# A two-layer hybrid encoder: the chunked attention's queries and keys by a seven-fold block product through DRAM, and one item of filler to a differential step

## The chip, the cores and the metric

The kernel runs on one core of one Trainium2 chip. The metric is the device time in microseconds of one execution. Before the change three runs gave 1897.2, 1899.48 and 1903.69 us, median 1899.48 us.

## The reference, cut to what matters

`x` has one batch of 512 rows of 1024 channels. Two layers follow each other; each has a token mixer of three branches on the same input, and a gated feed-forward net. All of it is float32.

```python
def _token_mixer(x, w_in, ...):
    rq, rk, rv, rg, cq, ck, cv, dq, dk, dv, gate = split(x @ w_in)   # widths below
    a = _retention(rq, rk, rv, rg) @ w_branch_a          # 4 heads
    b = _chunk_attention(cq, ck, cv, rel_bias) @ w_branch_b   # 8 heads of 64
    c = _diff_attention(dq, dk, dv, lam) @ w_branch_c    # 4 heads, 2 score maps of 64 each
    y = sigmoid(gate[0]) * a + sigmoid(gate[1]) * b + sigmoid(gate[2]) * c
    return y @ w_out
```

`cq`, `ck`, `cv`, `dq`, `dk` and `dv` are 512 columns wide, each gate 1024. In the chunked attention a chunk of 64 queries sees its own and the eight chunks before it, with a bias by clipped distance, a softmax and a product with the values. In the differential attention queries and keys are first turned by rotary positions; each head makes two softmax maps, subtracts the second times lambda from the first, multiplies by the values and normalises each row.

## The kernel before, in words

**Numbers.** A float32 operand is carried as two parts, a high one (a rounded copy, made by ACT) and a low one (the remainder, made by DVE); names end in `h` and `l`. A product is three matmuls into one PSUM bank, high by high, high by low, low by high (`mm3`, L122 to L125). Weights come as float32 by DMA into one of four staging buffers (`st`) and are split into `wh` and `wl` (class `Wt`, L128 to L157; the cast L155 is ACT's, the subtraction L156 DVE's), each in two halves. Three buffers of each sort hold the weights of three items at a time (`AHEAD` is 3). Most other tiles come from a pool of 61 slots of 128x512.

**Items and groups.** The mixer is written as a list of items (the table at L1095 to L1115 of before). An item is one weight, or a few, with the matmuls on it: nearly always two halves of 24 matmuls each. Behind an item's name stand groups of steps. Each call of `between` takes the next group: the first group runs between the halves of the item, the second at its end. So PE's order is the order of this table, and every other engine has its work queued in the order in which the table emits it; a scheduler moves instructions a little within that. When an item is emitted, the weights of the next ones are fetched and split, so their casts stand in ACT's and DVE's queues about two items early, and each waits until the buffer of an older weight has been read for the last time.

**Products of block matrices.** `u_two` (L716) computes two projections of 512 columns each by seven block products in place of eight (items `a` and `c` set up the operands; the items `m1, m2, y, x, g, h, v` are the products). An item has 48 matmuls 256 columns wide. It is used for the values of both attentions (`w`: CV and DV) and for the retention's values and gates (`p`, `q`). What `w` makes is stored in DRAM (`v_away`) and fetched again ahead of use (`v_back`).

**Queries and keys.** `u_cqk(p)` projects the queries and keys of one pair of chunked heads, as two halves of 24 matmuls 512 columns wide, four items a layer; `QK.set_q` and `set_k` (L361 on) split them into `qs`, `ks` and `kl`. `u_dqk(h)` does this for a differential head, with the rotary between (`rotary`, L345 on: four copies of 32 rows by ACT, L352, and three operations by DVE, L354 to L356).

**Steps.** `s_c1, s_c2, s_c3` are the steps of a chunked head: scores (L387, L388), row operation (DVE L402), exponentials (ACT L404), normalisation (DVE L899); transposes and split; product with the values (L924) and output `ob` (L926, L927 and the split). For a differential head `s_d0` makes scores and exponentials of one map, `s_d1` at its second map the combination `dE` (DVE, L964 to L970), `s_d2` the transposes (`ptr`) and their split, `s_d3` the product with the values (`pdo`), squares, POOL's power (L1011) and scalings (L1014), `s_d4` the transposes `pdt` and the output `oc`. `c(i)` and `d(i)` put them into groups, so that the steps of neighbouring heads overlap. Before, an odd step `d(2h+1)` and the next even one had an item with no steps between them (`u_dqk(1)`, `u_dqk(2)`, `u_dqk(3)`).

**Gates and branches.** `u_gate` projects 256 columns of a gate; the gates in `EARLY` (six of twelve) go to DRAM (`th`) and come back in `gate_of`. `u_branch(br, i)` multiplies a branch's output (`oa`, `ob`, `oc`) by its weight and adds it, gated, to the sum (L1065, L1069).

Of the kernel before, what the change touches and what calls it, by code (L numbers as in the profile page):

```python
# [12 lines left out]
F32 = mybir.dt.float32  # L13
# [4 lines left out]
P = 128  # L18
# [26 lines left out]
EARLY = [(0, 0), (0, 1), (0, 2), (0, 3), (2, 0), (2, 1)]  # L45
# [12 lines left out]
def trunk(ctx, tc, x_in, xT_in, w_in, ret_norm_g, da_norm_g, lq1, lk1, lq2, lk2, w_a, w_b, w_c, b_merge, w_out,  # L58
# [68 lines left out]
    class Wt:  # L127


        def __init__(self, pieces, nk, later=False):  # L130
# [230 lines left out]
    class QK:  # L361
# [21 lines left out]

        def scores(self, ps, j, nt):

            w, n = P * (nt + 1), slice(P * nt, P * nt + P)
            nc.tensor.matmul(ps[:, :w], self.q[j][:, n], self.k[j][:, :w], start=True, stop=False)  # L387
            nc.tensor.matmul(ps[:, :w], self.q[j][:, n], self.kl[j][:, :w], start=False, stop=True)  # L388
# [134 lines left out]

    def run_items():
        ready, at = [], 0

        def fetch():
            nonlocal at
            specs, at = items[at][0], at + 1
            ready.append([])  # L530
            if at == 1:
                ready[-1] += first_blocks(*specs)
                return
            for sp in specs:
                ready[-1].append(sp() if callable(sp) else Wt(*sp))

        for i, (specs, fn, groups) in enumerate(items):
            while at <= i or (at < len(items) and sum(map(len, ready)) < AHEAD):
                fetch()
# [37 lines left out]
    def layer(l):  # L577
# [138 lines left out]
        def u_two(left, right, left_done, right_done):  # L716
# [5 lines left out]
            def it(name, use):  # L722
                def fn(wt):
                    for j in range(2):
                        use(j, functools.partial(product, xq, name, j, wt))
# [158 lines left out]
        def s_c1(h):  # L884
            def fn():
# [168 lines left out]

        def u_branch(br, i):
# [3 lines left out]
            def fn(wt):  # L1059
                act = (oa, ob, oc)[br]  # L1060
                for j in range(2):
                    d = 2 * i + j
                    t = gate_of(br, d)
                    ps = proj_T(act, wt, P * j, nk=nk)
                    nc.vector.scalar_tensor_tensor(t, t, 1.0, ps, op0=ALU.add, op1=ALU.mult)  # L1065
                    if br == 0:
                        acc[d] = t
                    else:
                        nc.vector.tensor_add(acc[d], acc[d], t)  # L1069
                    if br == 2:  # L1070
                        mg[d] = Pair("mg")
                        split(mg[d], acc.pop(d), scale=0.5)
                    between()
            return [([w[:, 256 * i:256 * i + 256]], nk)], fn

# [17 lines left out]

        w, p, q = u_two(CV, DV, v_away(cv, 64), v_away(dv, 128, -1.0)), u_rvg(0), u_rvg(1)
        for (specs, fn), *groups in [  # L1095
            (u_first(), [w["a"]]), (u_gate(0, 1), [w["c"], s_q(0)], [s_q(1)]), (u_gate(0, 2), [s_q(2)], [s_q(3)]),
            (w["m1"],), (w["m2"], [lam]), (w["y"],), (w["x"],), (w["g"],), (u_gate(0, 3), [p["a"]], [s_dh(0)]), (w["h"],),
            (w["v"], [p["c"]]),
            (p["m1"], [], [s_r1(0)]), (p["m2"], [s_dh(1)]), (p["y"], [], [s_r1(1)]), (p["x"],), (p["g"],),
            (u_rqk(rq, RQ, 1), [q["a"]]), (p["h"],), (p["v"], [q["c"]]),  # L1100
            (q["m1"], [], [s_r2(0)]), (u_rqk(rk, RK, 1), [s_r2(1)], [s_r3(0)]), (q["m2"], [], [s_r3(1)]), (q["y"], [s_dh(2)]),
            (q["x"], [], [s_r1(2)]), (q["g"], [s_dh(3)]), (u_cqk(0), [], [s_r1(3)]), (q["h"],), (q["v"],),
            (u_gate(2, 0), [s_r2(2)], [s_r2(3), s_r3(2)]), (u_cqk(1), [s_r3(3)] + c(0)[0], c(0)[1]),
# [411 lines left out]
```

## Time and profile before

| | |
|---|---|
| median of the three runs | 1899.48 us |
| the profiled execution's own time | 1898.38 us |
| its span | 1896.5 us |
| granted TensorE clock, mean | 0.999 |
| PE, DVE, ACT, POOL busy | 99%, 72%, 50%, 6% |
| DMA | 297.84 MB, mean 157 GB/s |
| waits of PE in all | 14 us |

A row of the groups has the line, the engine, the operation, the tiles written and read, their shape, the count, then busy us and the mean ns of one, then the idle time of the engine ahead of them and what released it. A row of the windows has the stretch in us from the span's start, its length, and for PE, PEld, DVE, ACT and POOL the busy us with the number of instructions, then the granted clock, the mean busy share of the DMA engines and GB/s. A row of the timeline has start, length, engine, line, operation, tiles. In the first layer the differential steps run from about 399 to 534 us, the products of the third branch to 556 us; the second layer repeats them some 940 us later.

### The profile page before, as it was taken

How to read it: one execution, taken by the hardware profiler on the slowest of the kernel's cores; microseconds unless marked ns; L12 is line 12 of the kernel's file. 1: busy time of each engine (PE TensorE's matmuls, PEld its weight loads, DVE VectorE, ACT ScalarE, POOL GpSimd, SP SyncE). 2: the span in 40 equal slices, each digit the busy share in tenths (PEclk: the TensorE clock that was granted, in tenths of full speed). 3: DMA queues.
4: the chain of work that ended last, by engine and by line, in shares of the span. 5: the costliest groups of instructions: out<-in, count | busy, mean ns of one | idle time of the engine just before them, and what ended most of it. 6: DMA issues, size and time to landing. Idle time of an engine off the chain costs nothing. (4 is left out here: it accounts for less than half of the span.)

```text
span 1896.5 us, 26422 instructions
## 1 busy us (share of the span) xinstructions
PE 1873.9 (99%) x10354; PEld 1630.4 (86%) x10354; DVE 1358.4 (72%) x2065; ACT 957.4 (50%) x1547; POOL 105.5 (6%) x117
## 2 busy tenths in 40 slices
PE   9999999999999999999999999999999999999998
PEld 7788888888888999988898888888888889999886
DVE  5877766667766877787587777566776678877866
ACT  4644555567644444444255546455765344444431
POOL 0000000000001000010000010000000010000100
PEclk9999999999999999999999999999999999999999
DMA  8685443332156387885546835433322654869851
GB/s 264 193 255 141 142 142 127 109 117 87 56 169 187 105 231 177 240 209 151 156 167 195 241 110 166 159 112 97 122 71 80 199 129 145 211 157 266 206 149 45
DMA packets 221745, 297.84 MB, mean 157 GB/s; under 512 B 9534, under 2 KB 116148, under 8 KB 221620
## 3 DMA queue, kind: packets, MB, share of 16 engines
q1 hardware_dynamic: 198388, 250.01, 39.9%
q0 software_dynamic: 23232, 46.14, 14.0%
q8 instruction: 81, 1.33, 0.3%
q14 instruction: 44, 0.36, 0.1%
HBM read 273.00 MB, written 23.12 MB: 156 GB/s over the span
## 5 line engine op out<-in xcount | busy, mean ns | idle before, releaser
L123 PE MATMUL pt<-xTh,wh 128*128 128x512 f32 (+1 forms) x1456 | 506.9, 349 | 1.3 <-ACT wh L261 1.3
L124 PE MATMUL pt<-xTl,wh 128*128 128x512 f32 (+1 forms) x1456 | 502.5, 345 | 2.1 <-DVE xTl L113 1.9
L125 PE MATMUL pt<-xTh,wl 128*128 128x512 f32 (+1 forms) x1456 | 502.1, 345 | 0.0
L262 DVE TENSOR_TENSOR wl<-st,wh 128x2048 fp32r<-128x2048 f32 x126 | 288.1, 2289 | 135.0 <-ACT wh L261 134.7
L261 ACT CAST wh<-st 128x2048 fp32r<-128x2048 f32 x126 | 240.0, 1910 | 227.4 <-PE pt L124 129.1
L124 PEld LDWEIGHTS pt<-xTl,wh 128*128 128x128 f32 x1456 | 276.1, 190 | 34.5 <-DVE xTl L113 2.3
L123 PEld LDWEIGHTS pt<-xTh,wh 128*128 128x128 f32 x1456 | 275.7, 190 | 34.8 <-ACT wh L261 1.7
L125 PEld LDWEIGHTS pt<-xTh,wl 128*128 128x128 f32 x1456 | 275.7, 189 | 34.0
L155 ACT CAST wh<-st 128x1024 fp32r<-128x1024 f32 (+1 forms) x204 | 188.1, 948 | 195.6 <-issue 71.1
L156 DVE TENSOR_TENSOR wl<-st,wh 128x1024 fp32r<-128x1024 f32 (+1 forms) x204 | 219.0, 1095 | 90.6 <-ACT wh L155 84.2
L123 PE MATMUL pf<-wh,hqh 128*128 128x512 f32 x224 | 87.5, 391 | 0.5 <-DVE z L1272 0.5
L124 PE MATMUL pf<-wl,hqh 128*128 128x512 f32 x224 | 87.2, 389 | 0.0
L125 PE MATMUL pf<-wh,hql 128*128 128x512 f32 x224 | 87.1, 390 | 0.0
L123 PE MATMUL pt<-s43h,wh 128*128 128x256 f32 x256 | 72.7, 284 | 2.6 <-ACT wh L261 2.6
L352 ACT COPY sw<-pt 32x512 f32<-32x512 f32 (+1 forms) x96 | 55.6, 579 | 34.8 <-PE pt L125 33.6
L123 PE MATMUL pt<-s12h,wh 128*128 128x256 f32 x256 | 72.4, 283 | 0.0
L124 PE MATMUL pt<-s12l,wh 128*128 128x256 f32 x256 | 72.4, 283 | 0.0
L125 PE MATMUL pt<-s12h,wl 128*128 128x256 f32 x256 | 72.4, 283 | 0.0
L124 PE MATMUL pt<-s43l,wh 128*128 128x256 f32 x256 | 72.4, 283 | 0.0
L125 PE MATMUL pt<-s43h,wl 128*128 128x256 f32 x256 | 72.4, 283 | 0.0
L123 PE MATMUL pf<-wh,xTh 128*128 128x512 f32 x144 | 56.3, 391 | 0.0
L125 PE MATMUL pf<-wh,xTl 128*128 128x512 f32 x144 | 56.2, 391 | 0.0
(284 smaller groups left out, 3834.6 us busy)
## 6 DMA issues: line engine op xcount, KB each, us to landing
st<-in_w_in SPq DMA_DIRECT2D x60, 1024.0 KB
st<-in_w_ffn_in SPq DMA_DIRECT2D x40, 1024.0 KB
st<-in_w_ffn_out SPq DMA_DIRECT2D x24, 1024.0 KB
st<-in_w_in SPq DMA_DIRECT2D x32, 512.0 KB
st<-in_w_ffn_in POOLq DMA_DIRECT2D x16, 1024.0 KB, 10.4
st<-in_w_ffn_out POOLq DMA_DIRECT2D x16, 1024.0 KB, 9.8
st<-in_w_in POOLq DMA_DIRECT2D x12, 1024.0 KB, 11.2
th<-th SPq DMA_DIRECT2D x48, 256.0 KB
```

The lines of the kernel that those rows point to most:

```text
L123: nc.tensor.matmul(ps, lh, rh, start=start, stop=False, skip_group_check=more)
L124: nc.tensor.matmul(ps, lh, rl, start=False, stop=False, skip_group_check=more)
L125: nc.tensor.matmul(ps, ll, rh, start=False, stop=stop, skip_group_check=more)
L155: return [nc.scalar.copy(self.hi[:, a:b], self.st[:, a:b]), nc.vector.tensor_sub(self.lo[:, a:b], self.st[:, a:b], f(self.hi[:, a:b]))]
L156: nc.vector.tensor_sub(self.lo[:, a:b], self.st[:, a:b], f(self.hi[:, a:b]))]
L261: nc.scalar.copy(self.hi, st)
L262: nc.vector.tensor_sub(self.lo, st, f(self.hi))
L352: nc.scalar.copy(sw[half * b:half * b + half], ps[half * o:half * o + half])
```

## The change

1. `u_cqk` goes. A fourth block product, `e`, makes the queries and keys of all chunked heads (CQ and CK, 512 columns each) in seven items behind `w`, with `product_T`, which gives them transposed. `qk_away` splits the results and stores both parts in DRAM; `qk_back` makes the tiles of a head pair and fetches them with ten DMAs of 64x512 (`QK.fetch`).
2. A weight is split by one cast and one subtraction of its full width.
3. Eleven gates of twelve are `EARLY`, and the order of gates and branch items is another.
4. The normalisation of the chunked softmax is ACT's (L919 of after), not DVE's.
5. The differential steps stand one to an item: the item without steps between an odd step and the next even one is gone.
6. `u_branch_tail` emits the first two products of the third branch row by row, with the last steps of the last differential head and the last product of the second branch between the rows; it calls `fetch` itself, which is now outside `run_items`.

The core of the diff:

```diff
-EARLY = [(0, 0), (0, 1), (0, 2), (0, 3), (2, 0), (2, 1)]
+EARLY = [(br, i) for br in range(3) for i in range(4)][:-1]
...
-            h = max(nk // 2, 1)
-            for a in range(0, nk, h):
-                self.split(a, min(a + h, nk))
+            self.split(0, nk)
...
+        def fetch(self, away, c):
+            (qh, ql), (kh, kl) = away["q"], away["k"]
+            for j, own, oth in ((0, A, B), (1, B, A)):
+                for to, rows, src in ((self.q[j], own, qh), (self.q[j], oth, ql), (self.k[j], own, kh),
+                                      (self.k[j], oth, kh), (self.kl[j], own, kl)):
+                    nc.sync.dma_start(f(to[rows]), src[own, c])
...
-        def u_two(left, right, left_done, right_done):
+        def u_two(left, right, left_done, right_done, prod=product):
...
-        def u_cqk(p):
-            def fn(wt):
-                cqk[p] = QK()
-                cqk[p].set_q(proj_T(xT, wt, 0), -CA_DH ** -0.5)
-                between()
-                cqk[p].set_k(proj_T(xT, wt, P))
-            return [([wcols(CQ + P * p, P), wcols(CK + P * p, P)], KT)], fn
+        def qk_away(away, name, scale):
+            away[name] = [dram.tile([P, 2048], F32, name=f"{name}{part}{l}") for part in "hl"]
+            def done(i, src):
+                half, b = divmod(i, 2)
+                hi, lo = g(F32R, "qkh"), g(F32R, "qkl")
+                part_hi(hi, src, scale)
+                part_lo(lo, src, hi, scale)
+                for t, to in zip((hi, lo), away[name]):
+                    to = to.rearrange("p (q c) -> p q c", c=512)[:, 2 * b:2 * b + 2, 256 * half:256 * half + 256]
+                    nc.sync.dma_start(to, f(t).rearrange("p (q c) -> p q c", c=256))
+            return done
...
-                    nc.vector.tensor_scalar_mul(e, e, r[:, nt:nt + 1])
+                    nc.scalar.activation(e, e, AF.Identity, scale=r[:, nt:nt + 1])
...
+        def u_branch_tail(mids):
...
+                row(0, jobs[0] + jobs[1])
+                row(1, jobs[0] + jobs[1])
+                mids[0]()
+                row(2, jobs[0] + jobs[1])
+                last_b(0)
+                mids[1]()
+                last_b(1)
+                fetch()
+                th_ = [gate_of(2, d) for d in range(4)]
+                for i in range(2):
+                    row(3, jobs[i])
+                    if i == 0:
+                        fetch()
+                    for j in range(2):
+                        branch_done(2, 2 * i + j, th_[2 * i + j], jobs[i][j][2])
...
+        e = u_two(CQ, CK, qk_away(caw, "q", CA_DH ** -0.5), qk_away(caw, "k", None), product_T)
...
-            (u_dqk(0), *c(8)), (u_gate(1, 0), [v_back(dv)], [s_c3(7)] + d(0)[1]), (u_branch(1, 0), *d(1)), (u_dqk(1),),
-            (u_gate(1, 1), *d(2)), (u_branch(1, 1), *d(3)), (u_dqk(2),),
...
+            (u_gate(2, 0), c(8)[0], c(8)[1] + [v_back(dv)]), (u_dqk(1), [], [s_c3(7)] + d(0)[1]), (u_branch(1, 0), *d(1)),
+            (u_dqk(2), *d(2)), (u_branch(1, 1), *d(3)), (u_gate(2, 1), *d(4)), (u_dqk(3), *d(5)), (u_gate(2, 2), *d(6)),
+            (u_branch(1, 2), *d(7)), (u_gate(2, 3), [s_d4(2)], [s_d2(3)]), (u_branch_tail([s_d3(3), s_d4(3)]),),
```

Three places of ACT's queue, each before and after. The first is the start of the differential branch of the first layer, round the last output of the chunked attention. Before, in the order of the program; `th` is a gate, `cos` and `obh` the copy and cast of that output, `dE` the exponentials of the first head's two maps, `sw` and `qs` the next item's rotary copies and queries:

```order
L155 CAST wh_3606<-st_3605 128x1024 x2
L1035 ACTIVATE th_3562<-pt_3537,hb_354 128x512
L926 COPY cos_3573<-pco_3564 64x512
L107 CAST obh_3576<-cot_3408 128x512
L404 ACTIVATE dE_3580,sums_3583<-dE_3580,mx_3584 128x512
L404 ACTIVATE dE_3581,sums_3583<-dE_3581,mx_3584 128x384
L404 ACTIVATE dE_3582,sums_3583<-dE_3582,mx_3584 128x256
L404 ACTIVATE dE_3581,sums_3583<-dE_3581,mx_3584 128x128
L155 CAST wh_3677<-st_3676 128x512 x2
```

After, at the same place, with the weight of `u_branch(1, 1)` (`wh_4023`) first and then all of dqk1's queries and keys (`sw`, `qs`, `ks`):

```order
L153 CAST wh_4023<-st_4022 128x1024
L350 COPY sw_3928<-pt_3903 32x512 x4
L109 ACTIVATE qs_3895<-rot_3933 64x512
L109 ACTIVATE qs_3896<-rot_3933 64x512
L350 COPY sw_3966<-pt_3941 32x512 x4
L107 CAST ks_3897<-rot_3971 64x512 x2
L107 CAST ks_3898<-rot_3971 64x512 x2
L946 COPY cos_3990<-pco_3981 64x512
L107 CAST obh_3993<-cot_3806 128x512
L410 ACTIVATE dE_3997,sums_4000<-dE_3997,mx_4001 128x512
```

The copy and cast of the output moved behind the rotary of an item, where before they stood behind a gate's activation.

The second place is the third differential head, from its last projection to the cast of the older head's transposed maps (`dPh`). Before, with `wh_4416` a weight, `sw_4400` and `ks` the last item's keys, `th` a gate and `och` an output:

```order
L155 CAST wh_4416<-st_4415 128x1024
L352 COPY sw_4400<-pt_4375 32x512 x4
L155 CAST wh_4416<-st_4415 128x1024
L107 CAST ks_4331<-rot_4405 64x512 x2
L107 CAST ks_4332<-rot_4405 64x512 x2
L1035 ACTIVATE th_4448<-pt_4423,hb_354 128x512
L109 ACTIVATE och_4455<-pdt_4450,colv_352 128x512
L107 CAST dPh_4459<-ptr_4464 128x512
```

After:

```order
L153 CAST wh_4640<-st_4639 128x2048
L350 COPY sw_4591<-pt_4566 32x512 x4
L107 CAST ks_4481<-rot_4596 64x512 x2
L107 CAST ks_4482<-rot_4596 64x512 x2
L410 ACTIVATE dE_4606,sums_4609<-dE_4606,mx_4610 128x512
L1055 ACTIVATE th_4670<-pt_4645,hb_362 128x512
L410 ACTIVATE dE_4607,sums_4609<-dE_4607,mx_4610 128x384
L410 ACTIVATE dE_4608,sums_4609<-dE_4608,mx_4610 128x256
L410 ACTIVATE dE_4607,sums_4609<-dE_4607,mx_4610 128x128
L109 ACTIVATE och_4679<-pdt_4674,colv_360 128x512
L107 CAST dPh_4683<-ptr_4688 128x512
```

The four exponentials of the head's second map moved in between the keys and the transposed maps, where before an item without steps stood.

The third place is the second differential head, at its two maps. Before, with `wh_4210` a gate's weight, `dE_4184` to `dE_4186` the even map, `do` and `junk` the first head's output and its squares:

```order
L155 CAST wh_4210<-st_4209 128x1024
L404 ACTIVATE dE_4184,sums_4187<-dE_4184,mx_4188 128x512
L404 ACTIVATE dE_4185,sums_4187<-dE_4185,mx_4188 128x384
L404 ACTIVATE dE_4186,sums_4187<-dE_4186,mx_4188 128x256
L404 ACTIVATE dE_4185,sums_4187<-dE_4185,mx_4188 128x128
L1002 COPY do_4233<-pdo_4235 128x256
```

After, with `dE_4211` to `dE_4213` the even map of the second head, `dE_4318` its odd one, and `wh_4352` a gate's weight whose buffer `u_branch(1, 1)` reads before:

```order
L410 ACTIVATE dE_4211,sums_4214<-dE_4211,mx_4215 128x512
L153 CAST wh_4352<-st_4351 128x2048
L410 ACTIVATE dE_4212,sums_4214<-dE_4212,mx_4215 128x384
L410 ACTIVATE dE_4213,sums_4214<-dE_4213,mx_4215 128x256
L410 ACTIVATE dE_4212,sums_4214<-dE_4212,mx_4215 128x128
L1022 COPY do_4261<-pdo_4263 128x256
L1022 COPY do_4261<-pdo_4272 128x256
L1026 ACTIVATE junk_4262,ss_4260<-do_4261 128x128 x4
L410 ACTIVATE dE_4318,sums_4321<-dE_4318,mx_4322 128x512
```

The cast moved in between the even map's exponentials, and is one of the weight's full width.

More of the change, by code (lines that the diff above doesn't have):

```diff
@@ L522, in between, with fetch @@
                 fn()
-    def run_items():
[L525 to L535, printed above, removed]
+    ready, at = [], [0]
+    def fetch():
+        specs = items[at[0]][0]
+        at[0] += 1
+        ready.append([])
+        if at[0] == 1:
+            ready[-1] += first_blocks(*specs)
+            return
+        for sp in specs:
+            ready[-1].append(sp() if callable(sp) else Wt(*sp))
+    def run_items():
         for i, (specs, fn, groups) in enumerate(items):
-            while at <= i or (at < len(items) and sum(map(len, ready)) < AHEAD):
+            while at[0] <= i or (at[0] < len(items) and sum(map(len, ready)) < AHEAD):
                 fetch()
@@ L724, in fn @@
                     for j in range(2):
[L725 removed]
+                        use(j, functools.partial(prod, xq, name, j, wt))
                         between()
@@ L867, in layer, with qk_back, fn @@
         ob = [None] * 4
-        def u_cqk(p):
-            def fn(wt):
-                cqk[p] = QK()
-                cqk[p].set_q(proj_T(xT, wt, 0), -CA_DH ** -0.5)
-                between()
-                cqk[p].set_k(proj_T(xT, wt, P))
-            return [([wcols(CQ + P * p, P), wcols(CK + P * p, P)], KT)], fn
+        def qk_away(away, name, scale):
[9 more added lines that the diff above has]
+            return done
+        def qk_back(qk, away, p):
+            def fn():
+                qk[p] = QK()
+                qk[p].fetch(away, slice(512 * p, 512 * p + 512))
+            return fn
         def bias_table(h):
@@ L1053, in u_gate, with branch_done @@
             return [([wcols(GATE + D * br + 256 * i, 256)], KT)], fn
+        def branch_done(br, d, t, ps):
+            nc.vector.scalar_tensor_tensor(t, t, 1.0, ps, op0=ALU.add, op1=ALU.mult)
+            if br == 0:
+                acc[d] = t
+            else:
+                nc.vector.tensor_add(acc[d], acc[d], t)
+            if br == 2:
+                mg[d] = Pair("mg")
+                split(mg[d], acc.pop(d), scale=0.5)
         def u_branch(br, i):
@@ L1063, in fn, with row, last_b @@
                     t = gate_of(br, d)
[L1064 to L1072, printed above, removed]
+                    branch_done(br, d, t, proj_T(act, wt, P * j, nk=nk))
                     between()
             return [([w[:, 256 * i:256 * i + 256]], nk)], fn
+        def u_branch_tail(mids):
+            def fn(wb, *wts):
+                jobs = [[(wt, P * j, bank("pt")) for j in range(2)] for wt in wts]
+                def row(k, jobs):
+                    a = oc[k]
+                    for wt, c0, ps in jobs:
+                        mm3(ps, wt.hi[:, k, c0:c0 + P], wt.lo[:, k, c0:c0 + P], a.hi, a.lo, k == 0, k == 3)
+                def last_b(j):
+                    d = 6 + j
+                    branch_done(1, d, gate_of(1, d), proj_T(ob, wb, P * j, nk=4))
+                row(0, jobs[0] + jobs[1])
[13 more added lines that the diff above has]
+                        branch_done(2, 2 * i + j, th_[2 * i + j], jobs[i][j][2])
+            return [([w_b[l][:, 768:1024]], 4)] + [([w_c[l][:, 256 * i:256 * i + 256]], 4) for i in range(2)], fn
         def c(i):
```

26 lines of the change are left out of this document (13 added, 13 removed).

## The prediction

> **What bounds the kernel now.** I read the page first, then the waits of PE, then windows by stage, then the timeline round the start of the differential branch.
>
> ```profile
> span 1896.5 us, 26422 instructions
> PE 1873.9 (99%) x10354; PEld 1630.4 (86%) x10354; DVE 1358.4 (72%) x2065; ACT 957.4 (50%) x1547; POOL 105.5 (6%) x117
> PEclk9999999999999999999999999999999999999999
> ```
>
> The waits of PE, by who was waited for (us in total, times, longest); the two largest of eight rows:
>
> ```profile
> PE pf L123 <- ACT tu L731: 4.1, 3, 3.0
> PE pt L123 <- ACT wh L261: 3.9, 4, 1.3
> ```
>
> PE is busy for 99% of the span at full clock and waits 14 us in all (the eight rows). So matmul time is the span, and a change can win only by taking matmuls away; it can lose by making PE wait. The other engines have room on average, but the windows of the differential branch (busy us of PE, DVE, ACT) show where the room is small, and the price of a matmul can be read from a stretch of 512-wide and one of 256-wide ones:
>
> ```profile
> 400.00:431.00 31.00, 31.00 (x148) 26.01 (x147) 23.09 (x49) 20.59 (x43) 0.66 (x2) 1.00 0.34 107
> 431.00:465.00 34.00, 34.00 (x173) 28.97 (x173) 25.38 (x56) 23.59 (x53) 2.09 (x3) 1.00 0.24 78
> 465.00:498.00 33.00, 33.00 (x168) 28.05 (x167) 24.48 (x54) 22.59 (x53) 2.09 (x3) 1.00 0.15 49
> ...
> 408.00:418.00 10.00, 10.00 (x46) 8.26 (x45) 7.65 (x22) 5.01 (x13) 0.00 (x0) 1.00 0.39 106
> ...
> 700.00:712.00 12.00, 12.00 (x102) 12.00 (x101) 8.61 (x9) 5.86 (x6) 1.28 (x1) 1.00 0.88 266
> ```
>
> PE has no gap in the differential branch, though DVE and ACT are each busy for about 70% of it. Two of the counted matmuls reach over a window's ends: a 512-wide matmul starts every 10.00/44 = 0.227 us, a 256-wide one every 12.00/100 = 0.120 us.
>
> **The product by seven.** Per layer the change removes 4 items of 48 matmuls, 192 x 0.227 = 43.6 us, and adds 7 of 48, 336 x 0.120 = 40.3 us: 3.3 us less a layer, 6.5 us for the two. That is less than the eighth of the multiplications that it saves, since a 256-wide step costs more than half of a 512-wide one. All of it lies on PE, so on the path.
>
> What the seven products move beside them is seven loads of 1 MB (two of them accumulate) and 16 stores of 256 KB, 11.5 MB in 40.3 us. The nearest stage is that of the values' product by seven, which has the same loads and stores:
>
> ```profile
> 103.00:120.00 17.00, 17.00 (x77) 14.08 (x76) 11.14 (x14) 9.62 (x14) 1.28 (x1) 1.00 1.06 303
> ```
>
> There the DMA engines are full at 303 GB/s and PE still has no gap. At that rate the 11.5 MB take 38 us, two less than the product: I take 0, with 0 to 4 us a layer for the range (a 1 MB load that comes late by its own length, 1.05 MB at 303 GB/s, makes PE wait 3.5 us). The Trainium skill, page "DMA: Bandwidth & Descriptors", section "Specifications", gives about 358 GB/s of HBM for a core; by that figure the estimate is 32 us, and the stage would be further from its limit. The row says that with these packets it is nearer.
>
> The way back is 10 DMAs of 128 KB per head pair on SP's queue, and five more gates of 256 columns that go to DRAM and return. The rows of 400 to 498 above move 49 to 107 GB/s, a third of the row at 303 or less, so this is hidden; if the queue order makes a weight load late, it costs up to 1 us a layer. The normalisation moves 32 instructions a layer from DVE to ACT in a stage without PE waits: nothing, in either direction. A weight of 128x2048 is now split by one cast instead of two (rows below): 1.91 us instead of 2 x 1.05.
>
> **One filler a step.** Before, each pair of differential steps had three items (a projection of queries and keys, a gate, a branch product) round it; now there are two, and the steps of a head follow one item apart. What the queues need for a step is unchanged, what PE has to do meanwhile is a third less. Four places decide, alike in both layers. Durations for them, first of PE, ACT and DVE from the timeline (start, us):
>
> ```profile
> 406.18 0.39 PE L387 MATMUL psc<-ks,qs 128*128 128x512 f32 x1
> 406.98 0.28 PE L387 MATMUL psc<-ks,qs 128*128 128x256 f32 x1
> 407.39 0.44 PE L123 MATMUL pt<-xTh,wh 128*128 128x512 f32 x1
> ```
>
> ```profile
> 408.98 0.72 ACT L404 ACTIVATE dE<-dE,mx 128x512 f32<-128x512 f32 x1 [1.33 <-DVE mx L402]
> 410.79 0.39 ACT L404 ACTIVATE dE<-dE,mx 128x128 f32<-128x128 f32 x1
> 413.11 2.35 ACT L352 COPY sw<-pt 32x512 f32<-32x512 f32 x4 [1.84 <-PE pt L125]
> 417.60 1.28 ACT L109 ACTIVATE qs<-rot 64x512 fp32r<-64x512 f32 x2 [2.13 <-DVE rot L356]
> 418.91 1.05 ACT L155 CAST wh<-st 128x1024 fp32r<-128x1024 f32 x1
> ```
>
> ```profile
> 408.19 0.68 DVE L402 CUSTOM_DVE_ANT_0 dE<-psc,mask 128x512 f32<-128x512 f32 x1
> 409.62 0.28 DVE L402 CUSTOM_DVE_ANT_0 dE<-psc,mask 128x128 f32<-128x128 f32 x1
> 411.30 0.18 DVE L964 RECIPROCAL rec<-sums 128x4 f32<-128x4 f32 x1 [0.18 <-ACT dE L404]
> 411.98 1.94 DVE L970 SCALAR_TENSOR_TENSOR dE<-dE,rec 128x128 f32<-128x128 f32 x4
> ```
>
> And groups of the same branch by form (busy, mean ns), of ACT, DVE and POOL in turn, with two rows of the page for the undivided weight:
>
> ```profile
> L107 ACT CAST ks<-rot 64x512 fp32r<-64x512 f32 x12 | 7.4, 620 | 6.4 <-DVE rot L356 6.2
> L1006 ACT ACTIVATE junk<-do 128x128 f32<-128x128 f32 x16 | 4.8, 302 | 6.0 <-DVE do L1003 6.0
> L1002 ACT COPY do<-pdo 128x256 f32<-128x256 f32 x8 | 2.9, 364 | 0.4
> L107 ACT CAST obh<-cot 128x512 fp32r<-128x512 f32 x1 | 0.6, 621 | 1.0 <-DVE cot L927 1.0
> L926 ACT COPY cos<-pco 64x512 f32<-64x512 f32 x1 | 0.6, 584 | 0.0
> ```
>
> ```profile
> L1014 DVE TENSOR_SCALAR do<-do,rsr 128x128 f32<-128x128 f32 x16 | 4.4, 422 | 5.0 <-POOL rsr L1011 5.0
> L113 DVE TENSOR_TENSOR kl<-rot,ks 64x512 fp32r<-64x512 f32 x6 | 4.1, 687 | 4.0 <-ACT ks L107 4.0
> L113 DVE TENSOR_TENSOR obl<-cot,obh 128x512 fp32r<-128x512 f32 x1 | 0.7, 693 | 0.7 <-ACT obh L107 0.7
> L927 DVE TENSOR_TENSOR cot<-pco,cos 64x512 f32<-64x512 f32 x1 | 0.7, 685 | 0.0
> ```
>
> ```profile
> L1011 POOL TENSOR_TENSOR rsr<-ss,mhalf 128x4 f32<-128x4 f32 x4 | 4.0, 1007 | 124.3 <-DVE ss L1010 92.4 <-PE pt L125 32.0
> ```
>
> ```profile
> L262 DVE TENSOR_TENSOR wl<-st,wh 128x2048 fp32r<-128x2048 f32 x126 | 288.1, 2289 | 135.0 <-ACT wh L261 134.7
> L261 ACT CAST wh<-st 128x2048 fp32r<-128x2048 f32 x126 | 240.0, 1910 | 227.4 <-PE pt L124 129.1
> ```
>
> *First place, the last part of the chunked attention's output* (`ob[3]`, the operand of the first branch product). Now the item just before it projects queries and keys (dqk1). ACT's queue has, ahead of that item's rotary copies, the cast of the next branch weight (`wh_4023`), whose buffer comes free only with dqk1's last matmul; call that moment 0. The queries were ready 24 x 0.227 = 5.4 us earlier and stand still behind it. Then in a chain of ACT and DVE: cast 1.05; copies and rotary of the queries 417.60 - 413.11 = 4.5; their casts 1.28; copies and rotary of the keys 4.5; four casts of the keys 4 x 0.62 = 2.5; and only now the copy of the output 0.58, the product 0.69, its cast 0.62 and remainder 0.69. Sum 16.4 us. PE has until it needs that remainder: 8 matmuls of the last output, as wide as the scores' (407.39 - 406.18 = 1.2), the scores 1.2, 18 branch matmuls 4.1, four of the next scores 0.8 and one more 0.2: 7.5 us. PE waits 8.9 us. If the first rotary operation of each half overlaps the copies, it is 2 x 0.69 less, 7.5. I take 8.5.
>
> *Second, the first head's transposes.* From the end of its second scores (407.39) to the end of the combination (411.98 + 1.94) before took 6.5 us, and PE now has one half item, 24 x 0.227 = 5.4: 1 us (0 to 2).
>
> *Third, the second head.* ACT's queue (the third place in the rows of the change) has the cast of a gate weight (`wh_4352`) ahead of three exponentials of the even step; its buffer comes free with the last matmul of a branch product, moment 0. Then cast 1.9, three exponentials 1.5 (408.98 to 411.18 is 2.2 for four), two copies 0.7, four squares with their sums some 1.6, POOL's power 1.0, four scalings 4 x 0.42 less their overlap, 1.3: 8.0. Behind the scalings on DVE are a branch operation, the last score row and an addition (0.7 + 0.3 + 0.7), the reciprocals 411.98 - 411.30 = 0.7 and three of the four combinations (the widest comes last) 1.3: 11.7. PE has scores 1.2, 24 matmuls 5.4 and four transposes 0.4: 7.1. The wait is 4.6; where the scalings don't hold DVE's queue, the four exponentials behind the squares do (1.9 + 1.5 + 0.7 + 1.6 + 2.2 + 0.7 + 1.3 = 9.9), and it is 2.8. I take 4.5.
>
> *Fourth, the third head.* Moment 0 is the end of dqk3. ACT: the cast of a gate weight 1.9, with 2.3 of DVE for its remainder beside the copies; rotary to 6.3; two key casts 1.2 and the remainder 0.7, at 8.2; then the scores' row operations on DVE, 1.7 (408.19 to 409.90) and the other remainder 0.7, 10.6; the last exponential 0.4, reciprocals 0.7, three combinations 1.3: 13. PE has again 7.1. The wait is 6; if DVE can start the scores' rows before the rotary's end, 4.2 at the least. I take 5.
>
> Sum a layer 8.5 + 1 + 4.5 + 5 = 19, two layers 38 (bounds of the four: 7.5 + 0 + 2.8 + 4.2 = 14.5 and 8.9 + 2 + 5 + 6 = 22, doubled 29 and 44). The remade end (rows of the last branch products between the last head's steps) only fills PE where before no wait was, and I cost it at 0 to 1 us.
>
> The profiled execution took 1898.38 us, 1.9 more than its span and 1.1 less than the median 1899.48. So 1898.4 - 6.5 + 38 = 1930 us, with the bounds 1921 and 1936, and with 0 to 5 a layer for the loads and the queue 1921 to 1946. What a measurement can tell from no change is 0.3%, 5.7 us.
>
> **Rivals.** *Only the product counts.* The queues catch up and none of the four waits shows: 1898.4 - 6.5 = 1892, faster. For it: DVE 72% and ACT 50% busy, and no wait in the branch before. Against: the two casts at the places one and four stand in front of work that PE needs, and both wait for PE's own end of the item. It decides below 3.3 us of waits a layer, where the gain is eaten up. 0.10.
>
> *The product waits for its transfers, and the steps are covered.* At 4 us a layer 1898.4 - 6.5 + 8 = 1900, no change. For it is the share of 1.06; against it, PE's 17.00 of 17.00 under that share. 0.06.
>
> *Half the waits.* ACT and DVE have room enough that only the first place, which has the longest chain, waits: 1892 + 17 = 1909. For it: the third and fourth are sums of more steps with overlaps that I can't see. 0.14.
>
> *The waits lower the clock.* After each wait of 4.5 us or more, six in all, PE runs slower for a time. Eight steps at half speed are 8 x 0.227 = 1.8 us more, 11 in all: 1941. No row shows it: the longest wait of before is 3.0 us and all forty slices have full clock. 0.08. The Trainium skill has this as a rule against such gaps, page "TensorE: Matmul & The Clock Gate", section "Why this matters for your kernels": idle gaps over about 3 us take the array back to half its clock. No run here shows a gap long enough to agree or not.
>
> **How the numbers follow.** The forecast, all four waits at full clock, has the other 0.62. Faster is the first rival, 0.10; within 0.3% the second, 0.06; slower the rest, 0.84. The range leaves out those two rivals and takes in the third and fourth with their bounds: 1904 (the third at its lower end, 1892 + 2 x 7.5 = 1907, and 3 us less for such waits of before's 14 us as may go) to 1946.
>
> **What would show it.** In the changed profile PE should wait about 8 us twice for DVE's `obl`, and 4 to 6 us twice each for `dE` ahead of transposes; ACT should stand in `wh` waiting for PE just before. The seven products should have steps of 0.120 and no gaps. I am wrong in the mechanism if PE's waits stay at about 14 us in all, in size if the chain of one place overlaps, and in the product if PE waits there for `wh` behind a late load.

## The result, and the profile after

The changed kernel takes 2010.31 us (median of three, 2009.31 to 2013.35) against 1899.48: a ratio of 1.0583, 95% interval 1.0549 to 1.0618. The forecast was 1930 (1904 to 1946). The direction was right, but the kernel lost 111 us where 30 were forecast. The page of the changed kernel:

```profile
span 2008.4 us, 27184 instructions
PE 1906.9 (95%) x10642; PEld 1662.1 (83%) x10642; DVE 1347.1 (67%) x1910; ACT 970.7 (48%) x1500; POOL 110.4 (5%) x121
PEclk9999989998999999999999999999989999999999
```

PE is idle for 5% of the span where it was idle for 1%, and three slices have less than full clock. The waits of PE in the changed kernel (us in total, times, longest), the largest of 18 rows:

```profile
PE pt L123 <- DVE mx L408: 15.6, 4, 4.2
PE ptr L423 <- DVE dE L990: 14.4, 2, 7.2
PE pco L944 <- ACT cPh L107: 10.2, 2, 5.1
PE psc L393 <- DVE cot L947: 7.9, 2, 4.0
PE pt L123 <- DVE th L1076: 7.7, 2, 3.8
PE psc L393 <- DVE rot L352: 6.3, 2, 3.1
PE pf L123 <- ACT tw L738: 6.2, 2, 3.3
```

Nearly each stands there twice, once a layer. The rows sum to 91.8 us, those of before to 13.5: 78 us of the 112 that the span grew are waits, nearly all for ACT and DVE, and no row names a transfer. The rest is PE itself. The timeline of PE over one of these waits:

```profile
390.52 1.25 PE L423 MATMUL ptr<-ident,cE 128*128 128x128 f32 x10
395.98 0.79 PE L123 MATMUL pt<-xTh,wh 128*128 128x512 f32 x1 [4.21 <-DVE mx L408]
396.57 0.63 PE L124 MATMUL pt<-xTl,wh 128*128 128x512 f32 x1
397.00 0.63 PE L125 MATMUL pt<-xTh,wl 128*128 128x512 f32 x1
...
399.99 0.63 PE L123 MATMUL pt<-xTh,wh 128*128 128x512 f32 x1
400.41 0.57 PE L124 MATMUL pt<-xTl,wh 128*128 128x512 f32 x1
```

Behind the wait a 512-wide matmul starts every 0.427 us (396.57, 397.00, ...), not every 0.227. The windows round such waits show the granted clock (the column behind POOL; the first has this wait, the second two):

```profile
390.00:400.00 10.00, 5.79 (x23) 4.51 (x23) 4.78 (x12) 6.44 (x14) 0.00 (x0) 0.70 0.44 130
464.00:480.00 16.00, 8.90 (x28) 6.23 (x27) 10.82 (x28) 11.03 (x25) 1.04 (x2) 0.68 0.13 37
```

To split the growth I took each matmul's distance to the next from the timeline, less the step of its width (0.227 for 512 columns, 0.171, 0.120 and 0.109 for 384, 256 and 128): a distance over by more than 0.3 us that isn't a slow step is a wait, the rest over is slow steps. A wait comes out some 0.15 us longer by this measure than in the rows, and 0.4 where its first matmul is slow too; waits without a row beside them below are by this measure.

| us | before | after |
|---|---|---|
| sum of the steps | 1858.4 | 1852.0 |
| waits | 14.2 | 97.3 |
| slow steps | 19.6 | 54.6 |

So -6.4 for the product by seven, +83 of waits, +35 of slow matmuls: 112. (With the rows' 78 for the waits, the slow matmuls would be 40.) By place the waits of one layer are: differential branch 20.0 (7.7, 1.0, 4.0, 7.4), chunked attention 13.4 (3.8, 4.4, 5.2), retention stage 10.6 in the first layer and 8.0 in the second.

### The profile page after: what moved, and what is told of

Read it like the earlier page. It is cut to its first block, busy times and chain, and to the rows that moved or that the text cites. A ratio compares the mean times of both kernels' runs of the same rounds, so it can differ in the third digit from the quotient of the medians.

```text
span 2008.4 us, 27184 instructions
## 1 busy us (share of the span) xinstructions
PE 1906.9 (95%) x10642; PEld 1662.1 (83%) x10642; DVE 1347.1 (67%) x1910; ACT 970.7 (48%) x1500; POOL 110.4 (5%) x121
## 5 line engine op out<-in xcount | busy, mean ns | idle before, releaser
L123 PE MATMUL pt<-xTh,wh 128*128 128x256 f32 (+1 forms) x1424 | 488.9, 344 | 18.7 <-DVE mx L408 8.4
L124 PE MATMUL pt<-xTl,wh 128*128 128x256 f32 (+1 forms) x1424 | 483.6, 340 | 1.6 <-DVE xTl L113 1.6
L125 PE MATMUL pt<-xTh,wl 128*128 128x256 f32 (+1 forms) x1424 | 482.5, 339 | 0.0
L260 DVE TENSOR_TENSOR wl<-st,wh 128x2048 fp32r<-128x2048 f32 x140 | 320.1, 2289 | 133.0 <-ACT wh L259 132.5
L259 ACT CAST wh<-st 128x2048 fp32r<-128x2048 f32 x140 | 266.7, 1909 | 263.1 <-PE pt L124 122.1
L154 DVE TENSOR_TENSOR wl<-st,wh 128x2048 fp32r<-128x2048 f32 (+2 forms) x99 | 190.3, 1924 | 152.1 <-ACT wh L153 144.1
L153 ACT CAST wh<-st 128x2048 fp32r<-128x2048 f32 (+2 forms) x99 | 159.5, 1613 | 222.9 <-PE pt L124 126.8
L123 PE MATMUL pt<-s12h,wh 128*128 128x256 f32 x320 | 90.6, 283 | 0.0
L124 PE MATMUL pt<-s12l,wh 128*128 128x256 f32 x320 | 90.6, 283 | 0.0
L123 PEld LDWEIGHTS pt<-s43h,wh 128*128 128x128 f32 x320 | 61.4, 192 | 3.0 <-ACT wh L259 3.0
```

What stands on the lines that cost most here:

```text
L123: nc.tensor.matmul(ps, lh, rh, start=start, stop=False, skip_group_check=more)
L124: nc.tensor.matmul(ps, lh, rl, start=False, stop=False, skip_group_check=more)
L125: nc.tensor.matmul(ps, ll, rh, start=False, stop=stop, skip_group_check=more)
L153: return [nc.scalar.copy(self.hi[:, a:b], self.st[:, a:b]), nc.vector.tensor_sub(self.lo[:, a:b], self.st[:, a:b], f(self.hi[:, a:b]))]
L154: nc.vector.tensor_sub(self.lo[:, a:b], self.st[:, a:b], f(self.hi[:, a:b]))]
L259: nc.scalar.copy(self.hi, st)
```

## The experiments

All medians beside the kernel before as run with them (1896.5 to 1899.2 us).

**Casts and normalisation.** `a_halves`:

```diff
-            self.split(0, nk)
+            h = max(nk // 2, 1)
+            for a in range(0, nk, h):
+                self.split(a, min(a + h, nk))
```

> The changed kernel with one thing undone: a weight is again split in two halves. Theory one, a full-width cast and remainder (1.9 + 2.3 us) stand in ACT's and DVE's queues ahead of the rows of scores and make the waits of the chunked attention (3.8 and 4.4 us a layer) and part of those of the differential branch: PE's waits fall by 16 us or more in the two layers and, with the slow matmuls behind each, the time by 20 to 40 us. Rival, the steps have too little matmul work beside them whatever the cast's width: within 6 us of the changed kernel.

2007.58 us, ratio 1.0569 (1.0550 to 1.0588). Single waits moved (3.8 to 3.0, 4.4 to 2.5, but 5.2 to 7.1), their sum by the rows is 84.8. Theory one falls for the width of the cast. `a_norm`:

```diff
-                    nc.scalar.activation(e, e, AF.Identity, scale=r[:, nt:nt + 1])
+                    nc.vector.tensor_scalar_mul(e, e, r[:, nt:nt + 1])
```

> The changed kernel with one thing undone: DVE normalises the chunked softmax again. Theory one, the four normalisations on ACT (1.9 us for a head) hold up the copies of the rotary and the cast of the transposed map, and make the wait of 5.2 us a layer ahead of the last output: that wait falls to 3 or less, the time by 5 to 15 us. Rival, the wait comes from the rotary and the weight's cast ahead of that cast: no change beyond 6 us, and DVE, which has the remainder of the weights too, waits longer elsewhere.

2011.27 us, ratio 1.0590 (1.0574 to 1.0605). The wait ahead of `pco` is shorter, nearly as was expected (3.3 at the longest, 5.1 in the changed kernel):

```profile
PE pco L944 <- ACT cPh L107: 6.6, 2, 3.3
```

The time is the same: the normalisation is not what costs.

**The clock.** `b_gaps` is the kernel before with PE stopped eight times:

```diff
+        def stop_pe(ps, n):
+            x = g(name="stop")[:, :P]
+            tc.keep_in_program_order(nc.vector.tensor_copy(x, ps[:, :P]))
+            for _ in range(n):
+                tc.keep_in_program_order(nc.vector.tensor_scalar_mul(x, x, 1.0))
+            tc.keep_in_program_order(nc.tensor.transpose(bank("ptr")[:, :P], x, ident))
...
                         split(mg[d], acc.pop(d), scale=0.5)
+                        if j == 0:
+                            stop_pe(ps, (6, 18, 10, 14, 4, 24, 8, 12)[4 * l + i])
```

> The kernel before with eight stops of PE, between the halves of the last branch products, where DVE and ACT have little else: a chain of 4 to 24 small DVE operations on the first half's result, and a transpose that waits for it. Theory one, a wait alone lowers the clock: behind waits above about 3 us the matmuls run at half rate for 3 to 5 us (1.5 to 2.5 us lost each), behind shorter ones at full rate. Rival, the slow matmuls of the changed kernel come from what runs beside them (transfers, PSUM reads): behind these waits all run at 0.227 us.

1980.97 us, ratio 1.0430 (1.0409 to 1.0451), 82 us for eight stops. The waits by their row are 67.6 us; the timeline over the second, and the clock of a window behind it:

```profile
562.37 0.45 PE L1060 MATMUL ptr<-ident,stop 128*128 128x128 f32 x1 [13.60 <-DVE stop L1059]
...
563.05 0.63 PE L124 MATMUL pt<-ocl,wh 128*128 128x512 f32 x1
563.47 0.63 PE L125 MATMUL pt<-och,wl 128*128 128x512 f32 x1
...
565.18 0.59 PE L123 MATMUL pt<-och,wh 128*128 128x512 f32 x1
565.61 0.40 PE L124 MATMUL pt<-ocl,wh 128*128 128x512 f32 x1
```

```profile
562.00:566.00 4.00, 3.63 (x10) 2.94 (x11) 0.23 (x1) 0.00 (x0) 0.00 (x0) 0.55 0.00 0
```

With no transfer, no ACT and next to no DVE work the step is again 0.427 us, at a clock of 0.55. All eight waits (4.4 to 15.4 us) have such a stretch behind them, 1.4 to 2.7 us lost, the mean 2.0. The loss does not follow the wait's length: 1.7 us behind the shortest, 1.6 and 2.3 behind the two longest. So a wait alone does it. `b_gaps_short` has the stops 0, 1, 2, 3, 0, 1, 2, 3:

> The kernel of b_gaps with shorter stops (chains of 0 to 3 small operations behind the first half's gating), eight waits of some 2.5 to 4 us. Theory (a wait must last some 3 us for the clock to fall): behind waits under 3 us all matmuls at 0.227 us, behind those over it 1.4 to 2.7 us lost as in b_gaps. Rival: the loss falls off with the wait's length: less than 1 us behind waits of 3 to 4 us.

1958.13 us (one execution). Four waits came out as 5.3 to 5.5 us and two as 9.3, longer than I meant, all with 1.9 to 2.5 us lost; only two are near the edge, both 3.3 us. The windows over them, one in each layer:

```profile
536.00:545.00 9.00, 5.82 (x26) 4.55 (x26) 4.79 (x9) 1.86 (x4) 0.00 (x0) 1.00 0.43 146
1507.00:1516.00 9.00, 5.82 (x20) 4.34 (x19) 3.22 (x7) 1.47 (x3) 0.00 (x0) 0.81 0.44 147
```

The same wait once costs nothing and once 1.7 us. The Trainium skill, page "TensorE: Matmul & The Clock Gate", section "What's actually happening", says that the clock is halved after an idle window of about 3.4 us, and that the window runs freely. These runs agree in part. Every wait over 3.5 us was followed by about half rate, and the stretches at half clock in the changed kernel's trace last 3.4 us (nine), 6.8 (six) or 10.2 (two), as with a window of that length. But shorter waits were followed by half rate too, some of them of only 2 us, in which no window of 3.4 us fits, and there the measurement decides. One from the retention stage of the changed kernel, with the clock behind it:

```profile
257.57 0.58 PE L123 MATMUL psr<-rqkh 128*128 128x256 f32 x1 [2.00 <-DVE rtmp L794]
```

```profile
257.50:261.00 3.50, 3.43 (x9) 2.75 (x10) 2.55 (x3) 1.38 (x3) 0.52 (x1) 0.52 0.99 314
```

**Packing alone.** `b_packed2` is the kernel before with the differential steps one to an item, and some gates and branch items moved to give that order its operands (a first order, `b_packed`, used a gate ahead of the item that makes it and has no time):

```diff
-            (u_dqk(0), *c(8)), (u_gate(1, 0), [v_back(dv)], [s_c3(7)] + d(0)[1]), (u_branch(1, 0), *d(1)), (u_dqk(1),),
-            (u_gate(1, 1), *d(2)), (u_branch(1, 1), *d(3)), (u_dqk(2),),
...
+            (u_dqk(0), *c(8)), (u_gate(1, 0), [v_back(dv)]), (u_gate(1, 1),), (u_dqk(1), [], [s_c3(7)] + d(0)[1]),
+            (u_branch(1, 0), *d(1)), (u_dqk(2), *d(2)), (u_branch(1, 1), *d(3)), (u_gate(1, 2), *d(4)), (u_dqk(3), *d(5)),
+            (u_gate(1, 3), *d(6)), (u_branch(1, 2), *d(7)), (u_gate(2, 2), [s_d4(2)], [s_d2(3)]),
+            (u_branch(1, 3), [s_d3(3)], [s_d4(3)]), (u_gate(2, 3),),
```

> The kernel before with one thing done: the differential steps stand one to an item, as in the change, with two gates moved to give the order its operands. Nothing is left out. Theory of my prediction (the missing item between an odd step and the next even one makes the waits of the differential branch by itself): 15 to 20 us of waits a layer and some 1.9 us of slow matmuls behind each of 3 us or more, 1935 to 1955. Rival (it needs the cast of a weight to stand in front of the steps, and with halves it stands elsewhere): one or two waits a layer, under 1920.

1953.45 us, ratio 1.0295 (1.0279 to 1.0310), 55 us more, with divided weights and without the new product. PE's waits in the branch of its first layer:

```profile
PE ptr L417 <- DVE dE L970: 11.2, 3, 7.2
PE psc L387 <- DVE cot L927: 4.4, 1, 4.4
PE psc L387 <- DVE rot L354: 3.2, 1, 3.2
```

That is 18.8 us, and 17.9 in the second layer (18.9 by the rows in the changed kernel). Three of the waits (`rot`, `cot` and the longest for `dE`) stand where the changed kernel has them, with nearly the same lengths; the other 4.0 us here are ahead of transposes, where the changed kernel has 0.8 ahead of `pdo` and 3.8 ahead of a projection. The packing alone makes waits of this size.

**The fetch.** `a_cb_late`:

```diff
-            (u_branch(0, 0), [v_back(cv), cb(1)] + c(1)[0], c(1)[1]), (u_branch(0, 1), *c(2)),
+            (u_branch(0, 0), [v_back(cv)] + c(1)[0] + [cb(1)], c(1)[1]), (u_branch(0, 1), *c(2)),
...
-            (u_gate(1, 2), [cb(3)] + c(5)[0], c(5)[1]), (u_dqk(0), *c(6)), (u_gate(1, 3), *c(7)),
+            (u_gate(1, 2), c(5)[0] + [cb(3)], c(5)[1]), (u_dqk(0), *c(6)), (u_gate(1, 3), *c(7)),
```

> The changed kernel with one thing done: within its group, the fetch of a head pair's queries and keys is written behind the steps, not ahead of them. Theory: written ahead, it makes the scheduler put a weight's cast and remainder ahead of the rows of scores at two steps a layer (waits of 3.8 and 4.4 us); behind them, those two waits and the slow matmuls behind them go, 2 x (3.8 + 4.4 + 2 x 1.9) = 24 us. Rival: the transfers themselves, or the cover, make these waits: less than 6 us.

1993.16 us, ratio 1.0500 (1.0476 to 1.0523), 17 us less than the changed kernel, between theory (24) and rival. The row `pt <- DVE mx` is gone, a wait of 1.8 us stands near one of the two places of the first layer. How the two waits came about in the changed kernel is seen on ACT and DVE at the second of them (scores end at 385):

```profile
390.49 1.90 ACT L153 CAST wh<-st 128x2048 fp32r<-128x2048 f32 x1 [5.99 <-PE pt L124]
392.29 0.61 ACT L107 CAST obh<-cot 128x512 fp32r<-128x512 f32 x1
```

```profile
392.42 2.29 DVE L154 TENSOR_TENSOR wl<-st,wh 128x2048 fp32r<-128x2048 f32 x1 [7.21 <-ACT wh L153]
394.63 0.68 DVE L113 TENSOR_TENSOR obl<-cot,obh 128x512 fp32r<-128x512 f32 x1
395.23 0.68 DVE L408 CUSTOM_DVE_ANT_0 cE<-psc,tb 128x512 f32<-128x512 f32 x1
```

The row of scores waits in DVE's queue behind a weight's remainder, that for its cast, and the cast for the end of PE's item; then PE waits for the bank that the row reads. DVE was idle for 7.2 us with the row of scores ready from 385 on.

**The queue's order.** `a_pin`:

```diff
-            return [nc.scalar.copy(self.hi[:, a:b], self.st[:, a:b]),
-                    nc.vector.tensor_sub(self.lo[:, a:b], self.st[:, a:b], f(self.hi[:, a:b]))]
+            return [tc.keep_in_program_order(nc.scalar.copy(self.hi[:, a:b], self.st[:, a:b])),
+                    tc.keep_in_program_order(nc.vector.tensor_sub(self.lo[:, a:b], self.st[:, a:b], f(self.hi[:, a:b])))]
```

> The changed kernel with one thing done: the cast and the remainder of a weight are pinned in ACT's and DVE's queues to where the program writes them, behind the steps of the item before; in the changed kernel the scheduler has put several of them ahead of steps whose inputs PE delivers 5 to 6 us earlier. Nothing else differs. Theory one (the queue's order makes the waits): the two waits of 3.8 and 4.4 us in the chunked attention go, the first place of the differential branch falls from 7.7 to some 2, the others fall by about 2 each; PE's waits fall by 35 us or more in all, with them six or more stretches of slow matmuls, and the time by 45 to 80 us, to 1930 to 1965. Rival (too little matmul work beside the steps): the work of a step is the same, the waits move to other places, and the time changes by less than 15 us.

2023.05 us, ratio 1.0657 (1.0641 to 1.0673): slower. The two waits of the chunked attention fell below 1 us and the first place of the differential branch to 2.3, as theory one had it, but weights came late elsewhere:

```profile
PE pco L944 <- ACT cPh L107: 15.4, 5, 6.0
PE ptr L423 <- DVE dE L990: 15.0, 4, 4.6
PE pt L123 <- ACT wh L153: 14.2, 2, 8.9
```

So the order of a queue sets where a wait falls; the sum by the rows hardly moved (93.0), as the rival had it.

**The light step.** `a_dqk0`:

```diff
-            (u_gate(1, 2), [cb(3)] + c(5)[0], c(5)[1]), (u_dqk(0), *c(6)), (u_gate(1, 3), *c(7)),
-            (u_gate(2, 0), c(8)[0], c(8)[1] + [v_back(dv)]), (u_dqk(1), [], [s_c3(7)] + d(0)[1]), (u_branch(1, 0), *d(1)),
+            (u_gate(1, 2), [cb(3)] + c(5)[0], c(5)[1]), (u_gate(1, 3), *c(6)), (u_gate(2, 0), *c(7)),
+            (u_dqk(0), c(8)[0], c(8)[1] + [v_back(dv)]), (u_dqk(1), [], [s_c3(7)] + d(0)[1]), (u_branch(1, 0), *d(1)),
```

> The changed kernel with one thing done: the first query-and-key item of the differential branch (dqk0) stands two items later, at the light last step of the chunked attention as before the change, and not at a full step. Theory: a full step beside a rotary is too much for ACT, which makes the wait of 5.2 us ahead of the last outputs but one; it goes, with its 1.9 us of slow matmuls, 14 us for the two layers. Rival: the wait moves on to the next item, since the sum of the work is the same: under 6 us.

1999.59 us, ratio 1.0541 (1.0519 to 1.0563), 11 us less than the changed kernel, and the row `pco <- ACT cPh` is gone: a rotary beside a full step made that wait.

**The retention stage.** `a_rv` has its items and steps in the order of before:

```diff
-            (u_gate(0, 3), [], [s_r1(0)]), (p["m1"], [s_dh(1)]), (p["m2"], [], [s_r1(1)]), (p["y"],), (p["x"],),
...
+            (p["m1"], [], [s_r1(0)]), (p["m2"], [s_dh(1)]), (p["y"], [], [s_r1(1)]), (p["x"],), (p["g"],),
+            (u_rqk(rq, RQ, 1), [q["a"]]), (p["h"],), (p["v"], [q["c"]]),
...
+            (q["x"], [], [s_r1(2)]), (q["g"], [s_dh(3)]), (q["h"], [], [s_r1(3), cb(0)]), (q["v"], [], [s_c1(0)]),
```

> The changed kernel with one thing undone: the items and steps of the retention stand in the order of before, behind the new product. Theory: the change packs the retention's steps closer beside the short products (5.8 us an item), and makes the waits of 3.9, 1.0, 2.2 and 3.5 us in the first layer there and 1.3, 1.0, 2.1 and 3.1 in the second; they fall to under 1 us each, 15 to 20 us less with the slow matmuls. Rival: the stage now has one item less of queries and keys in it, and waits in either order: under 6 us, or worse.

2021.61 us, ratio 1.0653 (1.0626 to 1.0679). The stage's waits did fall to about 1 us each, but a new one came:

```profile
PE psc L393 <- DMA ks<-kh: 27.2, 2, 13.7
```

```profile
276.65 0.37 SPq L149 DMA_DIRECT2D st<-in_w_in  x1
277.07 0.59 SPq L388 DMA_DIRECT2D qs<-qh  x1
```

```profile
SPq L149 <- DVE wl L154: 14.3, 2, 10.7
```

The first fetch of queries and keys stood on SP's queue behind weight loads that wait for a staging buffer (L149, freed by a weight's remainder `wl`; SP's waits from 240 to 290 us), and the scores for the fetch. Without that wait the rows sum to 78.5 us, 13.3 less than the changed kernel's: an estimate of what the retention's order adds to PE's waits there.

**The items put right.** `a_filla` keeps the product, the full-width casts, the normalisation on ACT and the gates through DRAM, and orders the items of the attentions anew; for that it takes a gate item, `u_gate(0, 3)`, out of the retention stage. A second function, `u_rows`, is `u_branch_tail` without the second branch's last product. The lines added to the table, from the second gate of the second branch on:

```diff
+            (u_gate(1, 1), [s_r3(3), v_back(cv)] + c(1)[0] + [cb(1)], c(1)[1]),
+            (u_branch(0, 0), *c(2)), (u_branch(0, 1), c(3)[0] + [cb(2)], c(3)[1]),
+            (u_branch(0, 2), *c(4)), (u_gate(0, 3), c(5)[0] + [cb(3)], c(5)[1]),
+            (u_gate(1, 2), *c(6)), (u_branch(0, 3), *c(7)), (u_dqk(0), *c(8)), (u_gate(1, 3), [v_back(dv)], [s_c3(7)] + d(0)[1]),
+            (u_branch(1, 0), *d(1)), (u_dqk(1),), (u_gate(2, 0), *d(2)), (u_branch(1, 1), *d(3)), (u_dqk(2),),
+            (u_gate(2, 1), *d(4)), (u_branch(1, 2), *d(5)), (u_dqk(3),), (u_gate(2, 2), *d(6)),
+            (u_branch(1, 3), *d(7)), (u_gate(2, 3), [s_d4(2)], [s_d2(3)]), (u_rows([s_d3(3), s_d4(3)]),),
```

> The changed kernel with the order of its items remade: an item without steps stands again between an odd differential step and the next even one (dqk1, dqk2, dqk3), the first query-and-key item of the differential branch carries only the light last step of the chunked attention, as before, the fetches stand behind the steps, and a gate that stood in the retention stage is used as one of the items. The product by seven, the full-width casts, the normalisation on ACT and the gates through DRAM stay; nothing is left out. Theory (the missing cover makes the waits, the product itself is sound): the waits of the two attentions go, but for some 5 us a layer at the end, where rows of the third branch's products stand alone; the retention stage keeps its 5 to 10 us a layer. 1898 - 6.5 + 2 x (5 + 8 + 4 x 1.9) = about 1930, between 1905 and 1940. Rival (the product's transfers, the full-width casts or ACT's normalisation make part of the waits): over 1950.

1938.93 us, ratio 1.0218 (1.0199 to 1.0237), 71 us less than the changed kernel. From 390 to 530 us PE has no gap at full clock:

```profile
390.00:530.00 140.00, 140.00 (x693) 118.17 (x692) 98.99 (x197) 92.22 (x187) 6.25 (x10) 1.00 0.36 115
```

The 5 us that I expected at the end didn't come. What waits is the retention stage. `a_fillc1` gives that the order of `a_rv`, which is that of before, with the first fetch ahead of the loads. The places where it differs from `a_rv` there, cut out of their lines:

```diff
-... (q["y"], [s_dh(2)]),
+... (q["y"], [s_dh(2)], [cb(0)]),
...
-... (q["h"], [], [s_r1(3), cb(0)]), ...
+... (q["h"], [], [s_r1(3)]), ...
```

> The kernel of a_filla (the changed kernel with its items ordered so that the differential steps have an item without steps between them again, fetches behind the steps), with the retention's steps in the order of before as in a_rv, and the first fetch of queries and keys written four items earlier than there, ahead of the weight loads that it stood behind in SP's queue. Nothing is left out. Theory (all that the changed kernel loses is the order's waits and the slow matmuls behind them; the product itself is worth its 6.5 us): PE's waits fall to some 15 to 25 us in all, about those of before, and the time to 1890 to 1906. Rival (the short products have too much DVE and ACT work beside them in any order, or the transfers cost something of their own): waits of 2 to 4 us stay in the retention stage, 1915 to 1940.

1907.51 us, ratio 1.0053 (1.0038 to 1.0068); a little outside what the theory gave, with 22.4 us of waits by the rows, inside it. `a_fillc1h` is the same with divided weights (the diff of `a_halves`):

> The kernel of a_fillc1 with weights split in two halves again. Theory: the waits that are left in the retention stage (3.2 and 2.4 us in the first layer, 2.7 in the second) stand behind a remainder of 2.3 us on DVE; with pieces of 1.2 us they fall to 1 or 2 us and end the slow matmuls behind them: 5 to 12 us less than a_fillc1, 1896 to 1903. Rival: they come from the bank's copies behind the retention's casts, whatever the pieces: within 4 us of a_fillc1.

1905.72 us, ratio 1.0039 (1.0022 to 1.0056): within 4 us, so the rival. Its waits by the rows are 20.7 us (13.5 before), the largest:

```profile
PE pf L123 <- ACT tw L740: 5.3, 2, 2.9
PE px L482 <- DVE z L473: 4.2, 2, 2.3
```

By the steps it has -6.4 for the product, +7.4 of waits and +6.5 of slow matmuls, 7.5 us more than before, as measured (6.7). Which of the parts that it keeps makes these is not shown. No order that I ran beats the kernel before.

## Why the prediction was right and wrong

- *The product by seven, -6.5:* the sum of the steps fell by 6.4. Its transfers cost nothing there, as taken: in the changed kernel PE is busy for all of the stage from 92 to 160 us, at a DMA share of 1.01.

```profile
92.00:160.00 68.00, 68.00 (x464) 63.39 (x463) 43.73 (x42) 30.93 (x37) 3.85 (x3) 1.00 1.01 309
```

- *The differential branch, 19 a layer:* 20.0 came, and the packing alone gives 18.8 and 17.9 (`b_packed2`). The sum is near; of the ways to it two were right only in part. At the first place 8.5 was forecast and 7.7 came (two waits, 3.3 released by `rot` and 4.4 by `cot`). ACT had the order that was worked out: copies of the keys, their casts, then the copy and cast of the old output.

```profile
465.87 2.34 ACT L350 COPY sw<-pt 32x512 f32<-32x512 f32 x4
470.34 2.54 ACT L107 CAST ks<-rot 64x512 fp32r<-64x512 f32 x4 [2.14 <-DVE rot L354]
472.79 0.58 ACT L946 COPY cos<-pco 64x512 f32<-64x512 f32 x1
474.11 0.62 ACT L107 CAST obh<-cot 128x512 fp32r<-128x512 f32 x1 [0.75 <-DVE cot L947]
```

  But PE did not wait for `obl`, the sign that was given. It stood ahead of scores of the first head, which read neither of the two results that released them; what is left is the reuse of a PSUM bank that `rot` and `cot` read:

```profile
468.99 0.77 PE L393 MATMUL psc<-ks,qs 128*128 128x512 f32 x1 [3.15 <-DVE rot L352]
474.13 0.69 PE L393 MATMUL psc<-ks,qs 128*128 128x384 f32 x1 [3.96 <-DVE cot L947]
```

  At the second place 1 was forecast and none came. At the third 4.5 was forecast and 4.0 came (and 1.0 ahead of `pdo`), but not for `dE` ahead of transposes. PE stood ahead of the next projection, released by a branch operation that was behind the remainder of the gate weight on DVE. Those 2.29 us are not in the sum, so that its nearness is luck:

```profile
503.48 2.29 DVE L154 TENSOR_TENSOR wl<-st,wh 128x2048 fp32r<-128x2048 f32 x1 [1.41 <-ACT wh L153]
505.68 0.68 DVE L1076 SCALAR_TENSOR_TENSOR th<-th,pt 128x512 f32<-128x512 f32 x1
506.42 0.67 PE L123 MATMUL pt<-xTh,wh 128*128 128x512 f32 x1 [3.82 <-DVE th L1076]
```

  At the fourth 5 was forecast and 7.4 came, for `dE` ahead of transposes as worked out. It is beyond the upper bound of 6: the cast began 0.7 us after dqk3's end, a gate's activation stood between the exponentials, and the remainder of an older output ahead of the combinations, and the sum has none of these:

```profile
535.81 1.89 ACT L153 CAST wh<-st 128x2048 fp32r<-128x2048 f32 x1
545.72 0.69 ACT L1055 ACTIVATE th<-pt,hb 128x512 f32<-128x512 f32 x1
548.53 0.74 DVE L115 SCALAR_TENSOR_TENSOR ocl<-pdt,colv,och 128x512 fp32r<-128x512 f32 x1
```

- *The way back, "this is hidden":* the transfers were, their place in the program was not. Written ahead of a step, the fetch came with a queue order that cost 17 us (`a_cb_late`); why the scheduler reacts so was not tried. I had looked at two places of ACT's queue in the chunked attention's last step and at none of its first seven.
- *What the working left out:* the full step beside dqk0 (11 us, `a_dqk0`) and the retention's steps beside short products. The second I had not priced at all; the change moved those steps too. From `a_filla` to `a_fillc1` it is worth 31 us, but in an order whose waits there are half as long again as the changed kernel's (15.6 and 12.2 us in the two layers against 10.6 and 8.0); in the changed kernel itself it should be less, by `a_rv` some 13 us of waits and the slow matmuls behind them.
- *Casts of full width and the normalisation, nothing:* right, within 3 us (`a_halves`, `a_norm`).
- *The clock, a rival at 0.08:* it came behind every wait of 2 us and more. The price was right (1.8 us a wait, 2.0 measured), the chance and the number of waits were not: some 17 stretches with 35 us in place of six with 11. The row on which I had it at 0.08, a wait of 3.0 us without a slow stretch, could not speak on it: waits of this length, and of 2 us, come with such a stretch in some places and without it in others.

By the places, then: 38 forecast, 40 of waits came; 43 of waits at places that I didn't look at; 35 of clock on both. The step that failed is "Four places decide": the sum has no term for the chunked attention's first seven steps and the retention's steps, where some 43 us of waits came, and it left the clock, 35 us, to a rival. What bounds the kernel is how much matmul work stands beside each step, and the change took 43.6 us a layer of it out of the attentions and put the 40.3 where no step needed it; the reordered kernels get back 103 of the 111 us by giving the steps their cover again, with the product kept.

## What to carry to other kernels

A kernel whose first engine is busy for 99% hides its other engines' chains behind that work: before moving work from one stage to another, go through every stage that loses cover and every one that gets steps, not only the one that the change names. Price a wait of PE over some 3 us at its length plus 2 us, and count on that price for some waits of 2 us too. And read the order of each queue at all steps, since a transfer or a weight written a few lines earlier can set what stands ahead of a ready instruction.

## What the runs showed of the hardware

Behind a wait of 3.5 us or more PE ran 512-wide matmuls every 0.427 us instead of 0.227 for 3 to 6 us, whatever the wait's length up to 15.4 us, and also with next to nothing else at work on the core (`b_gaps`). Waits of 3.3 us did so in one of two otherwise equal places (`b_gaps_short`), and a wait of 2.0 us by its row did so in the changed kernel. In the traces of all these runs each stretch at half clock, but for the one at the kernel's end, lasted 3.41 us or two to five times that.
